# A hybrid decoder layer on one Trainium2 core: key preparation in two halves, gram masks with priority, side steps begun later, and one more dense unit in four chunk steps

## The chip, the cores and the metric

The program runs on one core of one Trainium2 chip. The core has five engines that work side by side, each through its own list of instructions in order: PE (TensorE: matrix products, with its weight loads PEld beside them), DVE (VectorE), ACT (ScalarE), POOL (GpSimd) and SP (SyncE, which here only issues transfers). They wait for one another by semaphores. Matrix products write to eight PSUM banks of 128 partitions by 512 fp32, everything else lies in SBUF. The metric is the time of one execution on the device in microseconds (us); lower is better.

## The reference, cut to what matters

One decoder layer, 512 tokens by 1024 channels in fp32, with a conditioning vector c that sets shifts, scales and gates:

```python
def rwkv7_time_mix(feat, ...):                    # group B, 8 heads of 64
    ...
    kk = kk / max(norm(kk), 1e-12)
    k = k * (1.0 + (a - 1.0) * k_a)
    def step(state, inp):
        r_t, w_t, k_t, v_t, kk_t, a_t = inp
        removed = einsum('bhvk,bhk->bhv', state, kk_t)
        state = state * w_t - removed * (kk_t * a_t) + v_t * k_t
        return state, einsum('bhvk,bhk->bhv', state, r_t)
    ...
# x1 = x + gate * (concat[fox_attention (A, 4 heads), rwkv7_time_mix (B), moba_attention (C, 4 heads)] @ w_out)
# all three from one projection of the normed and modulated x; then a gated MLP (width 2816) with a causal
# convolution of width 3, a gated residual add, and a last RMSNorm
```

## The kernel before

**Dense products.** Each fp32 matrix is split in a high and a low part, and a product is three matmuls of 128 x 512 (high by high, low by high, high by low; lines 459 to 461 for the input projection, 957 to 959 for the output projection). Three such matmuls are called a *dense unit* here. The class `Feed` holds the units of the input projection, and later of the output projection, as a queue. `feed.run(n)` puts the next n units at this place of the program, `feed.until(name)` as many as are needed for a named result. So units that depend on little stand between the steps of the recurrence, which depend on each other. Each unit also takes one *side step* from the list `feed.side` (line 115): 32 products of modulation weights on DVE (`mod2_steps`, line 434, each with a load of its own on SP's queue), then 16 more for the gates (`gate_steps`, lines 412 and 414) with their ends (`gate_parts`, lines 420 and 421; `gate_end`, lines 425 and 427).

**Order.** PE's instructions run in the order in which the code is written. On DVE, ACT and POOL a scheduler sets the order beforehand, by its own estimate of when an operand is ready and by priorities; `tc.high_priority(offset=n)` raises the operations inside it. On the chip each engine then keeps that order.

**Group B, gram stage (89.3 to 126.3 us).** The recurrence is worked in 8 chunks of 64 tokens, with the heads in four pairs j. For each pair `norm_cols(j)` spreads norms to a PSUM bank of the kind "at" (PE, line 529), `k_prep(j)` makes the key tiles from them on DVE (kk line 632, a 636, KR 637, BK 639, sq 641, BK 642, KR 643), `r_prep` (PE, line 665) and `k_cols` (POOL 653, ACT 655, PE transposes 658) use these, and `grams(j, par)` forms two products (PE, line 672), one in a bank "at" and one in a bank "ch". DVE multiplies each by a causal mask into AG (line 674, called the masks here), which frees the bank. There are 2 banks "at" and 3 "ch". Between the two grams of a pair stand F1 = 1 unit, behind them F2 = 2, 2, 2, 0 units. `norm_cols(j+2)` and `k_prep(j+2)` are written after the first gram of pair j.

**Chunk stage (185.5 to 269 us).** The loop over `cc` in `rwkv` carries the state `vs` through eight chunk steps. In each: px and py (PE, lines 1092 and 1098, which need the state), a softmax step of the attention and a unit ("a1"), pu (1108), copied back to `vs` by ACT (1109) and DVE (1110), again "a1", pn (1118), from which DVE makes the state of the next chunk in two additions with mp (line 1121; mp is POOL's, line 1102), the products of line 1124, and one unit. The attention steps put scores (1001, or 1003 and 1004, with 1005) in a bank "at", take their maximum on DVE (1008), exp on ACT (1010), 1011 and 1012 on DVE, then PE transposes (1019, in a bank "mm", like the units' sums) and ACT or DVE copies (1021). Operands of MoBA's scores are made in `split_head` (mqb line 732, mk line 735, on DVE). `scores` asks by `feed.until` for the units that it depends on.

**After that** the group norm (`gn_apply`), the rest of the attention, `put_y` (high part ACT line 936, low part POOL line 937), the output projection and, from 345 us on, the MLP, in which PE is never long without work.

Of the kernel before, what the change touches and what calls it, by code (L numbers as in the profile page):

```python
# [14 lines left out]
OP = mybir.AluOpType  # L15
# [3 lines left out]
P = 128  # L19
# [35 lines left out]
PAT = ['a1', 'a1', '1', '']  # L55
# [12 lines left out]
KO = 1  # L68
MP = ['', '2', '2']
PT = 3  # L70
GE = 3

SEVEN = (7, 9, 11, 13, 15)
NA = 16
# [66 lines left out]
def hybrid_trunk(ctx, tc, x, vecs, convs, mod_cols, mod_gates, in_first, in_cols, in_fox, in_moba, fox_f_bias, lora,  # L141
# [3 lines left out]
    V, S, G = nc.vector, nc.scalar, nc.gpsimd  # L145
# [4 lines left out]
    def c3(ap):  # L150
        return ap.rearrange("p (c t) -> p c t", t=C)
# [340 lines left out]
    with mix:  # L492
# [38 lines left out]
        with tc.tile_pool(name="prep", bufs=1) as pp:  # L531
# [98 lines left out]
            def k_prep(j):  # L630
                kk[j] = pp.tile([P, T], F32, name="kk", bufs=1)
                V.scalar_tensor_tensor(kk[j], kt[j], col("k_k", j), pnr[j], op0=OP.mult, op1=OP.mult)
                t1 = pp.tile([P, T], F32, name="t1", tag="sq", bufs=SQ)
                S.activation(t1, av[j], AF.Identity, scale=col("k_a", j), bias=omka[:, j:j + 1])
                G.tensor_tensor(kt[j], kt[j], t1, op=OP.mult)
                V.tensor_tensor(av[j], av[j], kk[j], op=OP.mult)
                V.tensor_tensor(KR[:, j, :, 0, :], c3(kk[j]), Pv[j][:, :, 0:64], op=OP.mult)
                BK[j] = pp.tile([P, 8, 3, 64], F32, name=f"BK{j}")
                V.tensor_tensor(BK[j][:, :, 0, :], c3(av[j]), c3(sv[j]), op=OP.mult)
                rk[j] = pp.tile([P, T], F32, name="sq", bufs=SQ)  # L640
                V.scalar_tensor_tensor(c3(rk[j]), KR[:, j, :, 1, :], col("r_k", j), c3(kt[j]), op0=OP.mult, op1=OP.mult)
                V.tensor_tensor(BK[j][:, :, 1, :], c3(kt[j]), c3(sv[j]), op=OP.mult)
                V.tensor_tensor(KR[:, j, :, 1, :], KR[:, j, :, 1, :], Pv[j][:, :, 1:65], op=OP.mult)
                S.copy(BK[j][H[1], :, 2, :], BK[j][H[1], :, 0, :])
# [22 lines left out]
            def grams(j, par):  # L667
                r = slice(64 * par, 64 * par + 64)
                for q in range(2):
                    pg = bank("ch" if q else "at", [P, 4, 2, 64])  # L670
                    for z in range(4):
                        mm(pg[:, z, :, :], BK[j][r, 4 * q + z, par:par + 2, :], KR[r, j, 4 * q + z, :, :],
                           start=True, stop=True)
                    V.tensor_tensor(AG[:, par, j, 4 * q:4 * q + 4, :].rearrange("p c (a t) -> p c a t", a=2), pg,
                                    mask[:, None, :, :].to_broadcast([P, 4, 2, 64]), op=OP.mult)

                for blk in range(2):
                    b = block(par, blk)
                    S.copy(AA[b, j], AG[b, par, j, :, 32 * blk:32 * blk + 32])


            norm_cols(0)
            k_prep(0)
            feed.until("r3")
            feed.run(LEAD[0])
            norm_cols(1)
# [3 lines left out]
            for j in range(4):  # L690
# [3 lines left out]
                k_cols(j, 0)  # L694
                for n, step in enumerate((lambda: grams(j, 0), lambda: feed.run(F1), lambda: k_cols(j, 1),
                                          lambda: grams(j, 1), lambda: feed.run(F2[j]), lambda: None)):
                    if n == KO and j < 2:
                        norm_cols(j + 2)
                        k_prep(j + 2)
                    step()  # L700
# [376 lines left out]


        v_tiles(0)
        feed.side += mod2_steps(w_m) + [mod2_end]  # L1080
        for half in range(2):
            feed.side += gate_steps(0, half, macc2, w_m) + [lambda half=half: gate_parts(0, half, m_part)]
            feed.side += [lambda: None] * GE + [lambda half=half: gate_end(0, half, bank("at"), g1b)]
# [1 line left out]
        for cc in range(NC_):  # L1085
# [42 lines left out]
            if cc > 5:  # L1128
                bonus(2 * cc - 12)
                bonus(2 * cc - 11)  # L1130
            fill(PAT[3])
        turn_bank[0] = "ch"
        gn_var(0)
        feed.run(G1)
# [443 lines left out]
```

## Time and profile before

| | |
|---|---|
| time, median of 3 runs | 745.96 us (744.57 to 748.39) |
| time of the profiled execution | 745.82 us |
| its span in the trace | 744.0 us, so 1.8 us lie around it |
| mean granted TensorE clock | 0.978 of full |
| PE, DVE, ACT, POOL busy in the span | 716.1, 484.3, 365.0, 311.6 us |

Busy time of PE holds waits that matmuls have inside them and stretches of slow clock, so that 96% isn't 96% of its peak. Idle time of another engine costs only what PE waits for it. The granted clock of a stretch stands in the column PEclk: 1.00 is 2.4 GHz, 0.50 is 1.2 GHz. In the rows by stretch that follow below, behind the stretch and its length stand PE, PEld, DVE, ACT and POOL, each as busy us and (x instructions), then PEclk, the share of the transfer engines and GB/s.

### The profile page before, as it was taken

To read this page: it belongs to the slowest core of one execution; us is meant where nothing else is said; L and a number is where in the kernel's file an instruction comes from. 1 tells how busy PE (TensorE), PEld (TensorE's weight loads), DVE (VectorE), ACT (ScalarE), POOL (GpSimd) and SP (SyncE) were. 2 spreads that over 40 slices of the span, in tenths; PEclk is the share of its full clock that TensorE was granted. 3 is DMA by queue.
4 is the path that set the end of the run, shared out by engine and by line. 5 is a ranking of instruction groups with operands and counts; after the bars stand their busy time and mean duration, and the time that the engine had idled before them with its cause. 6 is when DMAs were issued, how large, how long until landed. Compare 5 with 4: busy or idle time off the path is not lost.

```text
span 744.0 us, 11850 instructions
## 1 busy us (share of the span) xinstructions
PE 716.1 (96%) x4404; PEld 570.2 (77%) x4404; DVE 484.3 (65%) x833; ACT 365.0 (49%) x714; POOL 311.6 (42%) x264
## 2 busy tenths in 40 slices
PE   7999999999997999999999999999999999999996
PEld 5874767897665766677788888888888888888884
DVE  7957996876987567742639796788757683114104
ACT  8748655454432553645566545565563353223204
POOL 0023854664442312636576745454475432225210
PEclk9999989999977999999999999999999999999998
DMA  8941201237754141115234314323156633322203
GB/s 329 399 156 42 69 19 30 86 100 231 239 170 143 35 152 44 57 52 172 74 102 126 114 28 111 104 93 92 43 141 199 215 100 109 99 87 97 102 1 113
DMA packets 43021, 86.93 MB, mean 117 GB/s; under 512 B 5002, under 2 KB 5204, under 8 KB 42964
## 3 DMA queue, kind: packets, MB, share of 16 engines
q1 hardware_dynamic: 42963, 86.18, 36.0%
q8 instruction: 34, 0.56, 0.3%
q14 instruction: 24, 0.19, 0.1%
HBM read 84.05 MB, written 2.10 MB: 116 GB/s over the span
## 4 chain that ended last, share of the span: by engine, by line
PE 69%; DVE 15%; ACT 6%; issue 4%; POOL 3%; DMA 2%; SPq 0%; ACTq 0%; POOLq 0%; DVEq 0%
PE mm L459 3%; PE mm L460 3%; PE mm L461 2%; PE ch L378 2%; POOL w_lo L231 2%; PE ch L1188 2%; PE ch L1189 2%; PE ch L1187 2%; PE at L1315 2%; PE ch L1315 2%; PE at L1318 2%; PE at L1316 2%; DMA w_st<-in_w_up_dram 2%; PE ch L1318 2%; PE ch L1316 2%
## 5 line engine op out<-in xcount | busy, mean ns | idle before, releaser
L231 POOL TENSOR_TENSOR w_lo<-w_st,w_hi 128x512 fp32r<-128x512 f32 (+1 forms) x162 | 225.4, 1400 | 322.7 <-ACT w_hi L229 299.6
L229 ACT CAST w_hi<-w_st 128x512 fp32r<-128x512 f32 (+1 forms) x199 | 121.6, 618 | 157.1 <-PE at L1189 46.1
L231 DVE TENSOR_TENSOR w_lo<-w_st,w_hi 128x512 fp32r<-128x512 f32 x39 | 32.4, 832 | 72.8 <-ACT w_hi L229 72.7
L459 PE MATMUL mm<-h_hi,w_hi 128*128 128x512 f32 x104 | 49.4, 475 | 1.4 <-ACT ptr L1021 1.4
L460 PE MATMUL mm<-h_lo,w_hi 128*128 128x512 f32 x104 | 42.6, 410 | 0.0
L461 PE MATMUL mm<-h_hi,w_lo 128*128 128x512 f32 x104 | 42.6, 410 | 0.0
L1315 PE MATMUL ch<-h_hi,w_hi 128*128 128x512 f32 (+1 forms) x100 | 35.4, 363 | 0.7 <-ACT tm L1378 0.7
L1316 PE MATMUL ch<-h_hi,w_lo 128*128 128x512 f32 (+1 forms) x100 | 35.2, 361 | 0.0
L434 DVE SCALAR_TENSOR_TENSOR w_m<-w_m,cB 128x512 f32<-128x512 f32 x32 | 27.6, 886 | 9.3 <-DMA w_m<-in_mod_cols_dram 9.2
L1315 PE MATMUL at<-h_hi,w_hi 128*128 128x512 f32 (+1 forms) x88 | 32.4, 375 | 0.2 <-ACT tm L1378 0.2
L1316 PE MATMUL at<-h_hi,w_lo 128*128 128x512 f32 (+1 forms) x88 | 32.2, 372 | 0.0
L1008 DVE TENSOR_REDUCE mx<-at 128x1 f32<-128x128 f32 (+3 forms) x32 | 15.6, 488 | 18.9 <-PE at L1005 18.7
L1010 ACT ACTIVATE pr<-at,mx 128x128 f32<-128x128 f32 (+3 forms) x32 | 16.9, 527 | 21.8 <-DVE mx L1008 21.3
L459 PEld LDWEIGHTS mm<-h_hi,w_hi 128*128 128x128 f32 x104 | 20.6, 198 | 8.9 <-issue 3.1
L1444 ACT ACTIVATE tm<-tm 128x512 f32<-128x512 f32 x22 | 13.9, 632 | 27.5 <-DVE tm L1439 27.5
L1315 PE MATMUL mm<-h_hi,w_hi 128*128 128x512 f32 (+1 forms) x72 | 27.2, 382 | 0.0
L1316 PE MATMUL mm<-h_hi,w_lo 128*128 128x512 f32 (+1 forms) x72 | 27.1, 380 | 0.0
L461 PEld LDWEIGHTS mm<-h_hi,w_lo 128*128 128x128 f32 x104 | 20.6, 198 | 5.0
L1318 PE MATMUL ch<-h_lo,w_hi 128*128 128x512 f32 (+1 forms) x100 | 24.1, 363 | 0.0
L460 PEld LDWEIGHTS mm<-h_lo,w_hi 128*128 128x128 f32 x104 | 20.8, 200 | 2.4
L1445 DVE TENSOR_TENSOR tm<-tm 128x512 f32<-128x512 f32 x22 | 21.9, 993 | 1.0 <-ACT tm L1444 0.4
L1318 PE MATMUL at<-h_lo,w_hi 128*128 128x512 f32 (+1 forms) x88 | 22.2, 374 | 0.0
(667 smaller groups left out, 2049.3 us busy)
## 6 DMA issues: line engine op xcount, KB each, us to landing
w_st<-in_w_up_dram SPq DMA_DIRECT2D x88, 256.0 KB, 2.6
w_st<-in_w_down_dram SPq DMA_DIRECT2D x44, 256.0 KB, 2.6
wm<-in_mod_cols_dram SPq DMA_DIRECT2D x16, 512.0 KB, 10.3
w_m<-in_mod_cols_dram SPq DMA_DIRECT2D x32, 256.0 KB, 3.8
w_st<-in_in_cols_dram SPq DMA_DIRECT2D x30, 256.0 KB, 2.7
w_m<-in_mod_gates_dram SPq DMA_DIRECT2D x16, 256.0 KB, 2.9
w_st<-in_w_out_dram SPq DMA_DIRECT2D x16, 256.0 KB, 2.7
tm<-in_mod_gates_dram SPq DMA_DIRECT2D x16, 256.0 KB, 4.6
```

The costliest lines, as they stand in the source:

```text
L229: (V.tensor_copy if hv[0] else S.copy)(hi[:, :n], st[:, :n])
L231: e.tensor_tensor(lo[:, :n], st[:, :n], f32(hi[:, :n]), op=OP.subtract)
L434: V.scalar_tensor_tensor(wm, wm, 1.0, cB[:, cols], op0=OP.mult, op1=OP.mult, accum_out=acc2[:, z, k, half:half + 1])
L459: mm(out[0], hi[:, z, :], hT_hi[:, k, :], start=k == 0, stop=False)
L460: mm(out[0], hi[:, z, :], hT_lo[:, k, :], start=False, stop=False)
L461: mm(out[0], lo[:, z, :], hT_hi[:, k, :], start=False, stop=k == NK - 1)
L1008: V.reduce_max(mx[:, 0:1], s_ps[:, :n], axis=AX.X, negate=True)
L1010: S.activation(pr[:, :n], s_ps[:, :n], AF.Exp, bias=mx[:, 0:1], accum_out=mx[:, 1:2])
L1315: mm(o, hi[:, k, :], x[0][k], start=start and k == 0, stop=False, skip_group_check=not start)
L1316: mm(o, lo[:, k, :], x[0][k], start=False, stop=False, skip_group_check=not start)
L1318: mm(o, hi[:, k, :], x[1][k], start=False, stop=k == 3, skip_group_check=not start)
L1445: V.tensor_tensor(uv, ug, uv, op=OP.mult)
```

## The change

It does four things, and adds or removes no instruction:

1. `k_prep` is cut in two. kk, a and the first KR stay in it; BK, sq, the second BK, the second KR and the ACT copy become `k_prep2`. In the loop over the pairs `k_prep2(j+1)` is written after the first gram of pair j, and `norm_cols(j+2)` with the first half of pair j+2 ahead of the last units (n == 4), after the second gram.
2. The masks of line 674 get a priority offset of 60.
3. `feed.side` begins with 12 empty steps, so the 32 + 16 products are tied to units 12 places later.
4. Chunk steps 0 to 3 end with one more unit of the queue.

```diff
+AGP = 60
+SD = 12
...
                 V.tensor_tensor(KR[:, j, :, 0, :], c3(kk[j]), Pv[j][:, :, 0:64], op=OP.mult)
+
+            def k_prep2(j):
                 BK[j] = pp.tile([P, 8, 3, 64], F32, name=f"BK{j}")
...
-                    V.tensor_tensor(AG[:, par, j, 4 * q:4 * q + 4, :].rearrange("p c (a t) -> p c a t", a=2), pg,
-                                    mask[:, None, :, :].to_broadcast([P, 4, 2, 64]), op=OP.mult)
+                    with tc.high_priority(offset=AGP):
+                        V.tensor_tensor(AG[:, par, j, 4 * q:4 * q + 4, :].rearrange("p c (a t) -> p c a t", a=2), pg,
+                                        mask[:, None, :, :].to_broadcast([P, 4, 2, 64]), op=OP.mult)
...
             norm_cols(0)
             k_prep(0)
+            k_prep2(0)
...
-                    if n == KO and j < 2:
+
+                    if n == KO and j < 3:
+                        k_prep2(j + 1)
+                    if n == 4 and j < 2:
                         norm_cols(j + 2)
                         k_prep(j + 2)
...
-        feed.side += mod2_steps(w_m) + [mod2_end]
+        feed.side += [lambda: None] * SD + mod2_steps(w_m) + [mod2_end]
...
-            fill(PAT[3])
+
+            fill("1" if cc < 4 else PAT[3])
```

In the changed kernel the lines stand 2 to 10 lower (mask 674 is 679, pn's addition 1121 is 1130, the units 459 to 461 are 461 to 463).

DVE in the gram stage, from the first masks on. Before, two masks (AG) are followed by the seven products of pair 2's keys (kk to KR) and a product for kv, and only then by the masks of the second gram of pair 0:

```order
L674 TENSOR_TENSOR AG<-at,mask 128x512
L674 TENSOR_TENSOR AG<-ch,mask 128x512
L632 SCALAR_TENSOR_TENSOR kk<-kv,vec_107,at 128x512
L636 TENSOR_TENSOR a_731<-a_731,kk 128x512
L637 TENSOR_TENSOR KR<-kk,P_772 128x8x64
L639 TENSOR_TENSOR BK_945<-a_731,s_730 128x8x64
L641 SCALAR_TENSOR_TENSOR sq<-KR,vec_107,kv 128x512
L642 TENSOR_TENSOR BK_945<-kv,s_730 128x8x64
L643 TENSOR_TENSOR KR<-KR,P_772 128x8x64
L511 SCALAR_TENSOR_TENSOR kv<-mm,vec_107,kv 128x511
L674 TENSOR_TENSOR AG<-at,mask 128x512
L674 TENSOR_TENSOR AG<-ch,mask 128x512
```

In the changed kernel, the same place:

```order
L679 TENSOR_TENSOR AG<-at,mask 128x512
L679 TENSOR_TENSOR AG<-ch,mask 128x512
L679 TENSOR_TENSOR AG<-at,mask 128x512
L513 SCALAR_TENSOR_TENSOR kv<-mm,vec_107,kv 128x511
L679 TENSOR_TENSOR AG<-ch,mask 128x512
L634 SCALAR_TENSOR_TENSOR kk<-kv,vec_107,at 128x512
L638 TENSOR_TENSOR a_731<-a_731,kk 128x512
L639 TENSOR_TENSOR KR<-kk,P_772 128x8x64
L679 TENSOR_TENSOR AG<-at,mask 128x512
L643 TENSOR_TENSOR BK_1013<-a_731,s_730 128x8x64
L679 TENSOR_TENSOR AG<-ch,mask 128x512
L645 SCALAR_TENSOR_TENSOR sq<-KR,vec_107,kv 128x512
```

The masks of the second gram moved ahead of pair 2's products, and those of pair 1 stand between them. What lies ahead of these rows is as before: pair 1's seven products still precede the first mask. On PE the norms' matmul (line 529) of pairs 2 and 3 moved from the first unit between the two grams of a pair to behind the second gram.

PE from the end of chunk step 3 to the first score of step 4. Before, step 3 ends with one unit, and step 4 runs two units that `scores` asks for (mk_2432 comes out of the projection):

```order
L459 MATMUL mm<-h_hi,w_hi 128x512
L460 MATMUL mm<-h_lo,w_hi 128x512
L461 MATMUL mm<-h_hi,w_lo 128x512
L1092 MATMUL ch<-vs,AG 64x64 x8
L1098 MATMUL ch<-KR,vs 64x64 x8
L459 MATMUL mm<-h_hi,w_hi 128x512
L460 MATMUL mm<-h_lo,w_hi 128x512
L461 MATMUL mm<-h_hi,w_lo 128x512
L459 MATMUL mm<-h_hi,w_hi 128x512
L460 MATMUL mm<-h_lo,w_hi 128x512
L461 MATMUL mm<-h_hi,w_lo 128x512
L1003 MATMUL at<-mk_2432,mq_2152 128x128
```

In the changed kernel (mk_2352 is the same tile under another number):

```order
L461 MATMUL mm<-h_hi,w_hi 128x512
L462 MATMUL mm<-h_lo,w_hi 128x512
L463 MATMUL mm<-h_hi,w_lo 128x512
L461 MATMUL mm<-h_hi,w_hi 128x512
L462 MATMUL mm<-h_lo,w_hi 128x512
L463 MATMUL mm<-h_hi,w_lo 128x512
L1101 MATMUL ch<-vs,AG 64x64 x8
L1107 MATMUL ch<-KR,vs 64x64 x8
L1012 MATMUL at<-mk_2352,mq_2118 128x128
```

Step 3 now ends with two units and step 4 runs none ahead of its score. Steps 0, 1 and 2 also end with two where they had one, so the input projection is two units ahead from step 4 on. Behind the stage the output projection begins one attention step earlier, and two units fewer stand between the last attention products (1033) and the last units of the output projection.

DVE around the two additions that end chunk step 3. Before (macc are the gates' side steps, pr and mx the softmax):

```order
L1011 RECIPROCAL mx<-mx 128x1
L1121 TENSOR_TENSOR vs<-ch,mp 64x256
L1012 TENSOR_SCALAR pr<-pr,mx 128x512
L1121 TENSOR_TENSOR vs<-ch,mp 64x256
L414 SCALAR_TENSOR_TENSOR macc<-w_m,cact,macc 128x512 x3
L420 CAST m_part<-macc 128x512
L421 TENSOR_TENSOR m_part<-macc,m_part 128x512
L735 TENSOR_TENSOR mk_2432<-mm,mk_2432 64x512
```

In the changed kernel:

```order
L1020 RECIPROCAL mx<-mx 128x1
L1130 TENSOR_TENSOR vs<-ch,mp 64x256
L1021 TENSOR_SCALAR pr<-pr,mx 128x512
L744 TENSOR_TENSOR mk_2352<-mm,mk_2352 64x512
L1130 TENSOR_TENSOR vs<-ch,mp 64x256
L416 SCALAR_TENSOR_TENSOR macc<-w_m,cact,macc 128x512
L744 TENSOR_TENSOR mk_2355<-mm,mk_2355 64x512
```

The first mk product moved ahead of the second addition. In steps 0 to 3 the side steps moved little: 14 of the 32 products of line 434 stand ahead of the first maximum (1008) in both kernels, and at the copy of line 1110 in step 1 two more stand ahead of it than before.

## Rows read from the trace of the kernel before

**Rows 1.** The page: busy us by engine, share of the span, instructions.

```profile
PE 716.1 (96%) x4404; PEld 570.2 (77%) x4404; DVE 484.3 (65%) x833; ACT 365.0 (49%) x714; POOL 311.6 (42%) x264
```

**Rows 2.** Busy time by stretch: gram stage, then chunk steps 2, 3 and 4.

```profile
89.30:126.30 37.00, 34.18 (x230) 24.75 (x229) 31.72 (x39) 18.91 (x39) 19.31 (x15) 0.91 0.12 32
...
201.30:214.30 13.00, 12.20 (x101) 8.04 (x101) 10.28 (x25) 3.43 (x9) 5.84 (x6) 0.61 0.47 155
214.30:226.50 12.20, 10.21 (x122) 7.06 (x121) 11.99 (x26) 5.01 (x13) 6.79 (x9) 1.00 0.57 176
226.50:243.30 16.80, 14.40 (x121) 10.55 (x121) 12.64 (x24) 4.30 (x11) 3.76 (x4) 0.70 0.40 125
```

**Rows 3.** Busy time by stretch, the four that ran at the lower clock.

```profile
97.50:104.20 6.70, 6.70 (x19) 3.91 (x17) 6.60 (x8) 4.00 (x8) 2.73 (x2) 0.50 0.16 40
203.30:213.40 10.10, 9.34 (x68) 6.05 (x66) 7.46 (x19) 2.67 (x7) 3.69 (x4) 0.50 0.53 176
227.20:230.50 3.30, 3.30 (x22) 2.60 (x22) 3.11 (x5) 0.38 (x1) 1.44 (x2) 0.50 0.60 174
234.00:240.70 6.70, 6.27 (x39) 4.76 (x40) 4.16 (x10) 1.66 (x6) 0.00 (x0) 0.50 0.48 156
```

**Rows 4.** Timeline of PE, gram stage: start, duration, in brackets the wait before.

```profile
93.27 0.39 PE L460 MATMUL mm<-h_lo,w_hi 128*128 128x512 f32 x1
93.50 0.39 PE L461 MATMUL mm<-h_hi,w_lo 128*128 128x512 f32 x1
94.28 0.89 PE L658 MATMUL ch<-ident,BKs 64*128 64x64 f32 x8 [0.39 <-POOL BKs L653]
96.64 1.36 PE L672 MATMUL at<-KR,BK 64*128 64x128 f32 x8 [1.46 <-DVE AG L674]
...
100.23 0.63 PE L460 MATMUL mm<-h_lo,w_hi 128*128 128x512 f32 x1
...
115.17 1.16 PE L672 MATMUL ch<-KR,BK 64*128 64x128 f32 x8 [0.97 <-DVE AG L674]
```

**Rows 5.** Timeline of DVE, gram stage: a mask, and the next one.

```profile
96.50 0.68 DVE L674 TENSOR_TENSOR AG<-ch,mask 128x512 f32<-128x512 f32 x1
...
104.24 0.68 DVE L674 TENSOR_TENSOR AG<-at,mask 128x512 f32<-128x512 f32 x1
```

**Rows 6.** Waits of PE from 185 to 253 us: total, times, longest.

```profile
PE ch L1092 <- DVE vs L1121: 3.1, 4, 1.3
PE at L1003 <- DVE mk L735: 1.7, 1, 1.7
PE mm L459 <- ACT ptr L1021: 1.4, 2, 0.8
```

**Rows 7.** Timeline of PE, chunk stage: the state and a transpose in step 2, then waits behind step 3.

```profile
201.34 0.68 PE L1092 MATMUL ch<-vs,AG 128*64 128x64 f32 x14 [0.74 <-DVE vs L1121]
...
203.43 0.63 PE L1019 MATMUL mm<-ident,pr 128*128 128x128 f32 x2
...
225.53 0.30 PE L1092 MATMUL ch<-vs,AG 128*64 128x64 f32 x2 [1.34 <-DVE vs L1121]
226.48 0.68 PE L1092 MATMUL ch<-vs,AG 128*64 128x64 f32 x14 [0.65 <-DVE vs L1121]
```

**Rows 8.** Timeline of DVE and POOL, chunk stage.

```profile
194.19 1.10 DVE L434 SCALAR_TENSOR_TENSOR w_m<-w_m,cB 128x512 f32<-128x512 f32 x1
...
196.28 0.69 DVE L434 SCALAR_TENSOR_TENSOR w_m<-w_m,cB 128x512 f32<-128x512 f32 x1
...
192.64 2.10 POOL L1102 TENSOR_TENSOR mp<-vs,PC 64x256 f32<-64x256 f32 x2
```

**Rows 9.** Timeline of PE and POOL, a score and the first unit of the output projection.

```profile
299.06 0.91 PE L1001 MATMUL at<-fk,fq 66*128 66x384 f32 x2
...
300.92 0.50 PE L959 MATMUL mm<-w_hi,h_lo 128*128 128x512 f32 x1 [0.20 <-POOL h_lo L937]
...
300.14 6.09 POOL L937 TENSOR_TENSOR h_lo<-KR,h_hi 128x256 fp32r<-128x256 f32 x8
```

## The prediction

> **What bounds the kernel now.** I read the busy times first [rows 1]: PE works in 716.1 of 744.0 us, no other engine in more than 484.3. So a change that adds no instruction can only win what PE waits or loses to the lower clock, and both lie in few places. The busy time by stretch, with its clock column, then shows where: of the stretches that the change touches, the gram stage ran at a mean clock of 0.91, chunk step 2 at 0.61, step 4 at 0.70, and step 3 at 1.00 [rows 2]. Within these I looked for the stretches at exactly 0.50; there are four [rows 3]. What the lower clock does is seen in the same matmul of a unit: 0.39 us at 93.27, 0.63 at 100.23 [rows 4]. These times overlap with the next one: at full clock the next starts 0.23 us later (93.50), so a unit of three is worth about 0.7 us. Since half the clock takes twice the time for the same columns, I take half of the PE time in a stretch at 0.50 as lost.
>
> The list of waits then says what PE stood for. In the gram stage these are 0.39, 1.46 and 0.97 us [rows 4], 2.8 together. In the chunk stage they are 3.1 for the state of the next chunk (line 1121), 1.7 for mk and 1.4 for a softmax copy of ACT [rows 6], 6.2 together. The low stretches begin right behind such waits: the first after 0.39 and 1.46 in quick succession, the third after 1.34 and 0.65 [rows 3, 4, 7]; the wait of 0.97 at 115.17 was followed by no fall. So a wait costs itself, and sometimes several microseconds of half speed behind it. The clock cost 6.70 / 2 = 3.35 in the gram stage and (9.34 + 3.30 + 6.27) / 2 = 9.5 in the chunk stage [rows 3]. All that the change could win in these two stages is therefore 2.8 + 3.35 + 6.2 + 9.5 = 21.9 us.
>
> The Trainium skill, page TensorE: Matmul & The Clock Gate, Part 1, says that for modelling the ramp penalty is under 1% of a typical kernel span. By it the clock would be worth at most 7.4 us here; the four stretches show 12.8, and the sum goes by the stretches.
>
> **Gram stage: masks first.** At 96.64 PE waits to write a gram into a bank "at" that the first mask must empty. The norms' matmul of line 529 held the other bank "at" in between; it now comes after the second gram. So the "at" half of that gram starts when its transposes are through, about 95.2 (94.28 + 0.89). Its "ch" half needs a bank which the mask at 96.50 frees at about 97.2 [rows 4, 5]; the first half runs to about 96.2, so some 1.0 us of wait stands where 1.46 was. The seven products of pair 1 still precede the first mask, so this wait doesn't go. Then the change does help: before, the masks of the second gram waited behind pair 2's products from 97.2 to 104.24 [rows 5], and PE filled the time with units at half speed. Now they go at once, and the later ones stand between the products. The wait at 115.17 is of this kind too; I take its 0.97 as gone.
>
> The sum has 0.97 + 0.46 = 1.4 for the waits, and for the clock between 0 and 3.35: 0.39 and 1.0 stand behind each other, which lies between the 0.97 that passed and the 0.39 with 1.46 that did not. I take 0.6 of it, 2.0, and so a gain of **3.4 us** (1.2 to 4.8). More can't be had: DVE has 31.72 us of work in these 37.0 [rows 2], and a stage of 32.2 would leave it no room. What is late next is pair 2's own key products, which the masks now push back; POOL, with 19.31 us busy, covers that.
>
> The forward substitution that follows on DVE starts from the last masks and so moves with the stage; PE has units all through it. So the gain is not given back there.
>
> **Chunk stage: one more unit in steps 0 to 3.** A unit costs nothing as such, since it is taken from a later place. It is worth what it covers at the step's end, 0.7 us at full clock. Step by step:
> - Step 0: no wait there before; no gain.
> - Step 1: the two additions let PE wait 3.1 - 1.99 = 1.1 in all [rows 6, 7]; the unit covers 0.7, and as the rest was two short waits I count 0. But two more products of 0.69 [rows 8] stand ahead of the copy of line 1110, about 0.5 of a new wait before pn.
> - Step 2: the transposes of the softmax (1019) now want the bank that the second mqb product must empty. PE got to them 2.1 us after the second addition gave it the state (201.34 to 203.43) [rows 7]. Behind that addition DVE now has 1012, two mqb products and between them two of line 434; these take about 3.5 us, four at 0.69 (for mqb I take the duration of a product of line 434, which has as many columns) [rows 8] and 0.7 for 1012 and what POOL slows. So PE waits 1.4. Of the waits for copies (1.4 in two) I leave 0.4 here.
> - Step 3: DVE is the bound, 11.99 of 12.20 us busy [rows 2]. PE waited 1.99 [rows 7]. It gets there earlier if step 2 runs faster, and the mk product, taken at 0.69 like mqb, now stands between the two additions. The unit's 0.7 and this 0.69 cancel; for the earlier arrival I add 0.8, 2.8 in all. So the wait that the unit should hide grows where no DVE work goes away.
> - Step 4: the 1.7 for mk is gone, since that product comes early; PE's second copy wait stays at about 0.4.
>
> The waits after are 0.5 + 1.4 + 0.4 + 2.8 + 0.4 = 5.5, against 6.2. The clock decides: before it fell three times. In step 2 it fell behind waits which the unit largely covers, in step 4 a second time behind 1.7, which goes. A fall after step 3's 2.8 remains likely. I take about 8 us of PE time at 0.50, or 4.0 lost against 9.5. The gain is 0.7 + 5.5 = **6.2 us**; from 0.7, if all three falls stay, to 10.5, if none does and waits shrink no further.
>
> The rows bear on DVE's speed too. Beside POOL's products of line 1102 (2.10 for two) a product of line 434 takes 1.10 instead of 0.69 [rows 8], so about 0.4 each is lost when side steps lie there; the change leaves nearly as many there, so I count nothing. The Trainium skill, page SBUF — State Buffer, on the shared port pair, says that the loser fully blocks for the whole instruction. By it VectorE would stand still for the 2.10 and each such step would come 0.9 us later; the rows show both going on, slowed.
>
> **Side steps 12 places later.** The order of DVE shows almost the same products at the same places, because DVE and the loads set them, not the units. SP's loads of weights come a little earlier against these products' own loads. Cost and gain nothing; if the loads did come late, a product (0.69) would be late with them, which is inside the bounds of the chunk stage.
>
> **Tail.** Two units fewer stand at the output projection's start and end. Its first third matmul waited 0.20 for the low part from POOL [rows 9]. One attention step now stands behind that unit, of which the score alone takes 0.91, so PE gets there about 1 us earlier, while POOL's eight products there take 6.09 us from the same start [rows 9]. So the wait becomes 0.6 to 1.3, and with about 0.3 at the last unit I take a loss of **1.2 us** (0.3 to 2.5).
>
> **Sum.** Against the profiled execution: 745.82 - 3.4 - 6.2 + 1.2 = **737.4 us**. That execution lies 0.14 below the median of 745.96, so nothing is added for it.
>
> **Rivals.**
> - *No fall of the clock is left.* The chunk stage then gives 10.5, the gram stage 4.8, the tail costs 0.6: 731.1. For it: all falls stood behind waits over 1.1 us and most of these get shorter. Against: 2.8 in step 3.
> - *DVE bounds the chunk steps, so the units only move PE's waits.* DVE is busy 11.99 of 12.20 in step 3 and 12.64 of 16.80 in step 4 [rows 2]. PE then waits as long as before, the clock falls in steps 2 and 3, the stage gives about 1 and the gram stage 3.4 with a tail of 1.2: 742.6, at the edge of no change.
> - *Slower: the tail loses its cover.* The units moved forward are missing where the output projection waits for POOL. If that wait comes to more than about 1.5 us, as the waits that preceded a fall did, the clock falls there; a stretch such as those of 3.30 to 9.34 [rows 3] costs 1.7 to 4.7, with the wait 6. With the new bank wait in step 2 opening a second stretch (4.7) and only 1.4 won in the gram stage, and 1.7 for mk, the time is about 745.8 + 6 + 4.7 - 3.1 = 753. It decides from a tail wait of 1.5 on.
> - *The order doesn't do what it says.* The delay of the side steps is of that kind; if the masks too came no sooner, since the first one still waits behind seven products, only the chunk stage would pay: 745.82 - 6.2 + 1.2 = 740.8.
>
> **How the numbers follow.** A difference under 0.5%, 3.7 us, can hardly be told from none here; the borders are 742.2 and 749.7. Chances: my forecast (733 to 741) 0.47; no fall left 0.14; masks no help, at 740.8, 0.10; DVE as the bound 0.19, of which a good half lies beyond 742.2; slower or mishap in the tail 0.10, of which 0.07 beyond 749.7. So faster is 0.78, no change 0.15, slower 0.07. For 8 in 10 the range leaves out the fastest of the second case and the slow one: 730.5 to 744.
>
> **What would show it.** Right: in the gram stage masks between the key products, the wait at the second gram about 1.0 and for a "ch" bank, no 0.97 at pair 2, the stage near 33.5 us; in the chunk stage no wait for mk in step 4, full clock through step 2, and one fall behind step 3. Wrong: a stretch at 0.50 still from 97 on; waits at 1019 in step 2 over 2 us; a wait at line 1121's readers in step 3 well over 3 us; a low clock near 300 us; or DVE idle in steps 2 and 3, for then it is not the bound that I take it for.

## The result and the profile after

The changed kernel takes **737.69 us** (median of four, 735.14 to 739.35) against 745.27 for the kernel before in the same series; the ratio is 0.9889 (95% interval 0.9852 to 0.9926). A second series gave 738.86 and 0.9919 (0.9892 to 0.9946). So the gain is 0.8 to 1.1%, some 7 us, and the forecast of 737.4 was met. Its terms were not: that of the gram stage was 2.6 to 4 times too large, that of the chunk stage too small by 2.6 to 4.2 us.

The page of the changed kernel, engine times and the clock in 40 slices:

```profile
PE 709.4 (96%) x4404; PEld 565.1 (77%) x4404; DVE 479.2 (65%) x833; ACT 364.9 (50%) x714; POOL 310.5 (42%) x264
PEclk9999979999999999999999999999999999999999
```

All engines do the same work as in [rows 1]; PE is busy 6.7 us less for the same instructions. One dip of the clock is left, in the gram stage. The busy time by stretch (columns as in [rows 2]) shows the gram stage, then chunk steps 2, 3 and 4, then the only stretch at 0.50 between 60 and 360 us:

```profile
90.10:126.31 36.21, 35.35 (x230) 25.71 (x230) 30.77 (x39) 19.29 (x39) 19.32 (x15) 0.86 0.12 32
...
202.11:212.35 10.24, 9.15 (x107) 6.20 (x106) 9.99 (x25) 3.90 (x10) 5.95 (x6) 1.00 0.58 182
212.35:223.61 11.26, 10.82 (x120) 7.60 (x120) 10.99 (x26) 5.40 (x14) 5.14 (x8) 1.00 0.68 198
223.61:233.78 10.17, 8.73 (x116) 6.56 (x116) 9.85 (x20) 3.72 (x10) 4.75 (x6) 1.00 0.64 183
...
95.80:105.90 10.10, 10.04 (x37) 6.38 (x36) 7.28 (x10) 3.97 (x9) 4.54 (x3) 0.50 0.09 26
```

Against [rows 2, 3] the chunk steps run at 1.00, and steps 2 and 4 take 10.24 and 10.17 us instead of 13.00 and 16.80 (there the stretches were cut a little otherwise; from px to px, as cut here, they are 14.02 and 17.76). The gram stage is hardly shorter, and its stretch at 0.50 is longer than before: 10.10 us of which PE works 10.04.

The waits of PE from 185 to 253 us (total, times, longest), to be held against [rows 6]:

```profile
PE ch L1101 <- DVE vs L1130: 2.1, 4, 1.0
PE mm L1028 <- DVE mqb L741: 0.9, 1, 0.9
PE ch L1127 <- DVE vs L1119: 0.6, 1, 0.6
PE ch L1101 <- ACT vs L895: 0.5, 1, 0.5
PE ch L1107 <- DVE kv L923: 0.2, 1, 0.2
```

The waits for mk and for the softmax copies are gone, the two new ones (the bank behind mqb, the copy of line 1119 behind side steps) are there, and the state (line 1130, before 1121) costs 2.1 instead of 3.1.

To see where the time went I cut the span at five starts in the timeline of PE: first r_prep, first matmul after the grams, first px, last row of products (line 1124) of step 7, and the first matmul of the output projection's second half (line 966 before). For both kernels I have two profiles (the second ones are the control runs below):

| us | before | before, 2nd | after | after, 2nd |
|---|---|---|---|---|
| up to the gram stage | 89.31 | 89.80 | 90.10 | 89.50 |
| gram stage | 37.05 | 37.04 | 36.21 | 35.75 |
| up to the chunk stage | 59.16 | 59.16 | 59.16 | 59.16 |
| chunk stage | 81.94 | 79.05 | 72.97 | 71.64 |
| up to the output's second half | 74.67 | 74.64 | 74.29 | 75.29 |
| the rest | 401.87 | 401.81 | 403.77 | 402.06 |
| span | 744.0 | 741.5 | 736.5 | 733.4 |

The chunk stage gives 7 to 9 us although it now holds two units more (1.4 us), and the gram stage about 1. In the first profile the start and the rest, whose code the change leaves alone, take 2.7 of the gain back. The start varies by 0.8 us over all profiles, whatever the kernel. The rest isn't luck alone: in the four profiles of kernels without all four extra units (two of the kernel before, two of the experiments) it takes 401.7 to 402.1 us, in the ten with them 402.1 to 403.8. Each of these ten has a wait in the MLP that none of the four has, here that of the changed kernel:

```profile
PE mm L1236 <- DVE tm L1241: 0.3, 1, 0.3
```

So a small part of the gain is paid back there by the units; why the wait comes is open.

### The profile page after: what moved, and what is told of

The parts are those of the page before. It is cut to its first block, busy times and chain, and to the rows that moved or that the text cites. A ratio compares the mean times of both kernels' runs of the same rounds, so it can differ in the third digit from the quotient of the medians.

```text
span 736.5 us, 11843 instructions
## 1 busy us (share of the span) xinstructions
PE 709.4 (96%) x4404; PEld 565.1 (77%) x4404; DVE 479.2 (65%) x833; ACT 364.9 (50%) x714; POOL 310.5 (42%) x264
## 4 chain that ended last, share of the span: by engine, by line
PE 68%; DVE 13%; issue 5%; ACT 5%; DMA 4%; POOL 3%; SPq 0%; POOLq 0%; ACTq 0%; DVEq 0%
POOL w_lo L233 3%; PE mm L461 2%; PE ch L380 2%; PE ch L1198 2%; PE ch L1199 2%; PE ch L1197 2%; DMA w_m<-in_mod_cols_dram 2%; PE ch L1325 2%; DVE w_m L436 2%; PE mm L462 2%; PE at L1325 2%; PE ch L1328 2%; PE at L1328 2%; PE ch L1326 2%; PE at L1326 2%
## 5 line engine op out<-in xcount | busy, mean ns | idle before, releaser
L461 PE MATMUL mm<-h_hi,w_hi 128*128 128x512 f32 x104 | 47.5, 456 | 0.0
L436 DVE SCALAR_TENSOR_TENSOR w_m<-w_m,cB 128x512 f32<-128x512 f32 x32 | 27.1, 869 | 10.2 <-DMA w_m<-in_mod_cols_dram 10.0
L1325 PEld LDWEIGHTS ch<-h_hi,w_hi 128*128 128x128 f32 x100 | 18.8, 188 | 3.8 <-ACT tm L1388 0.6
```

Of the source, the lines that this page charges most:

```text
L436: V.scalar_tensor_tensor(wm, wm, 1.0, cB[:, cols], op0=OP.mult, op1=OP.mult, accum_out=acc2[:, z, k, half:half + 1])
L461: mm(out[0], hi[:, z, :], hT_hi[:, k, :], start=k == 0, stop=False)
L1325: mm(o, hi[:, k, :], x[0][k], start=start and k == 0, stop=False, skip_group_check=not start)
```

## The experiments

Each edit is to the changed kernel where nothing else is said. Times are medians, ratios are to the kernel before of the same series, whose medians were 744.87 to 746.17 us; a ratio need not be the quotient of the two medians.

**One part without the other: no extra unit.**

```diff
-            fill("1" if cc < 4 else PAT[3])
+            fill(PAT[3])
```

> The changed kernel with one unit at the end of chunk steps 0 to 3, as before; key halves, mask priority and delay stay. Theory (the extra unit made the chunk stage faster): only the gram stage's 0.8 us and the noise of the start are left, so 744 to 746; waits for the next state (line 1130) near 3 us in the chunk stage, and stretches at 0.50 in steps 2 to 4 again, 8 to 10 us lost. Rival (the gram stage's new order, or the delay, shifts the chunk steps out of the stalls): 737 to 739 with full clock in the chunk stage.

Measured: 740.69 us, ratio 0.9927 (0.9908 to 0.9946): neither 745 nor 738. In its profile step 4 (223 us on) is as bad as before, but step 2 ran at full clock without any unit:

```profile
200.03:210.29 10.26, 8.44 (x103) 5.68 (x103) 10.06 (x25) 4.09 (x11) 6.22 (x7) 1.00 0.58 194
222.20:240.29 18.09, 15.18 (x122) 10.87 (x122) 13.59 (x26) 4.21 (x11) 3.35 (x5) 0.62 0.42 128
...
PE ch L1101 <- DVE vs L1130: 3.3, 5, 1.3
PE mm L461 <- ACT ptr L1030: 1.8, 2, 1.1
PE at L1012 <- DVE mk L744: 1.6, 1, 1.6
```

So the waits of the stage came back as the theory of the unit has it. But more than half of the gain stayed (4.7 us against 745.34 in this series), which that theory hadn't.

**The extra unit alone**, put into the kernel before by the same line.

> The kernel before with the extra unit of chunk steps 0 to 3 alone. Theory of the unit: 736 to 739, chunk stage 73 us instead of 82 with no stretch at 0.50, gram stage 37 us as before with its waits of 1.46 and 0.97. Rival: 742 or more, falls of the clock in the chunk stage as before.

Measured: 740.93 us, ratio 0.9942 (0.9916 to 0.9968). Its chunk stage takes 75.6 us and its steps 2 and 4 look like those of the changed kernel:

```profile
207.62:217.57 9.95, 8.83 (x108) 6.01 (x107) 9.73 (x24) 3.91 (x10) 5.67 (x6) 1.00 0.56 184
228.81:238.99 10.18, 8.73 (x117) 6.56 (x116) 9.86 (x20) 3.72 (x10) 4.76 (x6) 1.00 0.59 185
```

In the chunk stage the unit does most of its work alone: 75.6 us against 81.9 and 79.1 before, and 73.0 and 71.6 in the changed kernel. PE still waits 2.0 us there for the copy of line 1110, where the changed kernel has 0.6 and 0.4. The product of the two ratios is 0.987, the ratio of the whole 0.989 to 0.992: the gain is the unit's and that of the other parts (called the gram part here), 4.4 and 4.7 us by the medians. Of the second, the profile without the unit shows some 1.7 us in the gram stage (35.39 against 37.05) and 1.1 between the chunk stage and the output's second half (73.54 against 74.67). There both profiles of the kernel before have two waits for the softmax that this one lacks:

```profile
PE ch L1019 <- DVE pr L1012: 0.6, 1, 0.6
PE ch L1019 <- DVE mx L1011: 0.5, 1, 0.5
```

The remaining 1.9 us aren't in a place that one profile shows.

**No delay of the side steps.**

```diff
-        feed.side += [lambda: None] * SD + mod2_steps(w_m) + [mod2_end]
+        feed.side += mod2_steps(w_m) + [mod2_end]
```

> The changed kernel without the 12 empty side steps. Theory (the delay moves next to nothing: on DVE only one addition of the gates changes its place, on PE two matmuls of the gates): 737.7 within 1.5, chunk stage 73 us at full clock. Rival (the delay takes side steps out of the crowded chunk steps): 740 or more with waits for the state over 3 us.

Measured: 736.52 us, ratio 0.9888 (0.9851 to 0.9926). The chunk stage takes 73.04 us with the same waits for the state (2.1). The 12 empty steps make no difference that is measured.

**No priority of the masks.**

```diff
-AGP = 60
+AGP = 0
```

> The changed kernel without the priority of the masks. By the order only two pairs of masks stand one product later and one mask changes place with a product of kv. Theory: no effect, 736.5 to 739, gram stage at equal clock as before within 0.3 us (32.2 us when 3.4 lost are taken off). Rival (the priority is what brings the masks forward): the wait of 0.97 at pair 2 returns, gram stage 1 us longer.

Measured: 736.84 us, ratio 0.9875 (0.9823 to 0.9927). The wait of 0.97 at pair 2 stays away; the gram stage keeps 0.8 and 0.9 of waits in pair 0. So it wasn't the priority that brought the masks forward; what is left is that pair 2's products are written after the second gram.

**Where the units stand, first: all four at the end of step 0.**

```diff
-            fill("1" if cc < 4 else PAT[3])
+            fill("4" if cc == 0 else PAT[3])
```

> The changed kernel with the four extra units all at the end of chunk step 0 and none at the ends of steps 1 to 3. Theory 1 (what counts is that the projection is two units ahead at step 4, so that mk is ready and no unit stands ahead of the scores): step 4 takes about 10 us as in the changed kernel (17.8 before), and the time is 737 to 739. Theory 2 (what counts is that a unit covers the wait for the state at the end of each step): waits for the state in steps 1 to 3 stay at 3 us, the clock falls in them, 740 to 742.

Measured: 745.50 us, ratio 0.9999 (0.9975 to 1.0023): the whole gain is gone, as much as the unit and the gram part bring together, though the gram stage takes 35.7 us in its profile. Neither theory had that. Its waits from 185 to 253 us, and steps 1, 3 and 4 by stretch:

```profile
PE mm L1028 <- DVE mqb L741: 3.9, 1, 3.9
PE mm L461 <- DVE mk L744: 2.8, 1, 2.8
PE ch L1101 <- DVE vs L1130: 0.8, 2, 0.4
...
193.84:207.10 13.26, 9.40 (x107) 7.02 (x106) 11.72 (x32) 4.95 (x15) 3.69 (x4) 0.87 0.73 234
216.20:231.24 15.04, 11.81 (x119) 8.15 (x118) 13.87 (x24) 6.09 (x15) 6.65 (x9) 0.89 0.50 142
231.24:239.96 8.72, 8.32 (x117) 6.30 (x116) 8.29 (x16) 3.14 (x9) 4.13 (x5) 1.00 0.33 93
```

Step 4 is faster still (8.72), as theory 1 says, but the projection's sums are finished before DVE can take them out of their banks "mm", and PE waits 3.9 and 2.8 for them in steps 1 and 3, whose mean clocks are 0.87 and 0.89. A unit that came before DVE could keep up was no filler here; it brought its tile's bank wait with it.

**Second: two units, at the ends of steps 2 and 3.**

```diff
-            fill("1" if cc < 4 else PAT[3])
+            fill("1" if cc in (2, 3) else PAT[3])
```

> The changed kernel with the extra unit at the ends of steps 2 and 3 alone, two instead of four; step 4 then needs none ahead of its scores. Theory 1 (two units ahead at step 4 is all): as the changed kernel within 1 us, step 4 about 10 us. Theory 2 (cover at each step's end): steps 1 and 2 wait about 1.1 and more again, the clock falls in step 2 in some executions, 739 to 741.

Measured: 738.40 us, ratio 0.9907 (0.9879 to 0.9936), between the two series of the changed kernel. Two units do what four do, within what is measured here. Step 4 took 14.53 us in its profile, with a wait of 1.8 for mk: not the 10 us of theory 1. By the profiles, chunk stage and the stretch up to the output's second half take 149.5 us together there, and 147.3 and 146.9 in the changed kernel, so the other two units may be worth 2 us there; the medians don't show it, and its rest (402.1 us) is among the short ones.

**The norms' matmul where it was**, with the key halves as changed.

```diff
+                    if n == KO and j < 2:
+                        norm_cols(j + 2)
                     if n == KO and j < 3:
                         k_prep2(j + 1)
                     if n == 4 and j < 2:
-                        norm_cols(j + 2)
                         k_prep(j + 2)
```

> The changed kernel with the norms' matmul (norm_cols of pairs 2 and 3) where it was, ahead of the unit between the grams; the key halves stay where the change put them. Theory (the matmul holds the bank at that the second gram wants): the wait for that bank returns, 1.2 to 1.5 us at the second gram of pair 0, and the wait for POOL falls from 0.8 to 0.4; the wait of 0.97 at pair 2 stays away. Gram stage 0.3 to 1 us longer at equal clock, 738 to 739. Rival (the order of masks and key products is all that counts): no wait over 1.1 there, same time as the changed kernel.

Measured: 737.85 us, ratio 0.9897 (0.9853 to 0.9941), as the changed kernel. The mechanism is as expected, seen in the waits of the gram stage:

```profile
PE at L676 <- DVE AG L679: 1.5, 1, 1.5
PE ch L662 <- POOL BKs L657: 0.4, 1, 0.4
```

The bank wait of 1.5 returns and the wait for POOL goes from 0.8 to 0.4, because this matmul (0.4 us) covered it. The sum is 1.9 either way, and the time is the same: its move bought nothing that is measured.

**Cover for POOL's wait: two units between the grams of pair 0.**

```diff
-                for n, step in enumerate((lambda: grams(j, 0), lambda: feed.run(F1), lambda: k_cols(j, 1),
-                                          lambda: grams(j, 1), lambda: feed.run(F2[j]), lambda: None)):
+                for n, step in enumerate((lambda: grams(j, 0), lambda: feed.run(F1 + (j == 0)), lambda: k_cols(j, 1),
+                                          lambda: grams(j, 1), lambda: feed.run(F2[j] - (j == 0)), lambda: None)):
```

> The changed kernel with two units between the grams of pair 0 and one behind, instead of one and two. Theory (the stretch at 0.50 from 95.5 to 106 follows the wait of 0.80 for POOL's BKs, and a unit of 0.7 covers it): wait under 0.2, no stretch at 0.50 in the gram stage, which takes about 31 us instead of 36.2; 732 to 733.5. Rival (the clock falls there for the small matmuls and the waits after them, whatever stands ahead): gram stage 35 to 37 us with a stretch at 0.50, 737 to 738.5.

Measured: 736.84 us, ratio 0.9890 (0.9864 to 0.9916), no gain over the changed kernel. The profile is of its longest execution (744.71 us, mean granted clock 0.982; the other nine had 0.986 to 0.995). In it the wait for POOL is gone, that of 1.1 for the first mask stays, and a stretch at 0.50 comes in which PE is busy throughout:

```profile
PE ch L676 <- DVE AG L679: 1.1, 1, 1.1
...
98.00:119.00 21.00, 21.00 (x83) 13.59 (x82) 12.20 (x17) 8.62 (x18) 5.05 (x6) 0.51 0.10 26
```

This profile doesn't tell what the other executions did. A mean clock of 0.986 over 739 us leaves at most 21 us at 0.50, and the last 2.4 to 4.9 us of every profile are of these, so none of the nine has room for a stretch that long; the three at 0.995 haven't even room for 6.8 us, the shortest seen in a gram stage. So in some executions the stretch was gone, and even these, at 733.67 to 735.66 us, didn't reach the 732 to 733.5 that the theory expected. But it was gone as well in one execution each of the run with the norms' matmul back (0.996) and of the unit alone (0.995), whose waits stand. So the cover isn't shown to be the reason.

**Both waits at once: a bank "mm" for the waiting half**, with the units as in the run above.

```diff
-                    pg = bank("ch" if q else "at", [P, 4, 2, 64])
+                    pg = bank(("mm" if j == 0 and par else "ch") if q else "at", [P, 4, 2, 64])
```

> The changed kernel with two units between the grams of pair 0 (one behind), and the second half of pair 0's second gram in a bank mm instead of ch, so that neither POOL's BKs nor the first masks let PE wait there. Theory (the stretch at 0.50 follows these two waits, 0.8 and 1.1): neither wait is left, no stretch at 0.50 in the gram stage, which takes 30 to 31 us; 733.5 to 735. Rival (the clock falls in the gram stage for the many small matmuls, or from wherever PE is held inside them): a stretch at 0.50 stays, the stage takes 33 us or more, the time stays within 1 of the changed kernel's 738.

Measured: 739.48 us, ratio 0.9940 (0.9905 to 0.9975). A miss: the extra unit finished a tile, and the bank "mm" was that tile's, whose product for kv waits on DVE. So it measured a longer wait in the same place, and a stretch at 0.50 of 23.5 us behind it (the profile is again of its longest execution, 747.41; the four at a mean clock of 0.979 to 0.981 took 745.0 to 747.4 us, the other eight, at 0.987 to 0.993, 736.8 to 740.1, with no room for such a stretch):

```profile
PE mm L676 <- DVE kv L513: 3.5, 1, 3.5
...
98.00:121.50 23.50, 21.82 (x82) 14.41 (x83) 12.37 (x17) 8.53 (x18) 4.88 (x5) 0.50 0.08 18
```

**Both waits at once, by units alone: one unit inside the second gram.**

```diff
                 for q in range(2):
+                    if q and par and j == 0:
+                        feed.run(1)
...
-                for n, step in enumerate((lambda: grams(j, 0), lambda: feed.run(F1), lambda: k_cols(j, 1),
-                                          lambda: grams(j, 1), lambda: feed.run(F2[j]), lambda: None)):
+                for n, step in enumerate((lambda: grams(j, 0), lambda: feed.run(F1 + (j == 0)), lambda: k_cols(j, 1),
+                                          lambda: grams(j, 1), lambda: feed.run(F2[j] - 2 * (j == 0)), lambda: None)):
```

> The changed kernel with the three units of pair 0 placed otherwise: two ahead of the second transposes (for POOL's BKs) and one between the two halves of the second gram (for the first masks), none behind. The banks stay as they are. Theory (the stretch at 0.50 follows the waits of 0.8 and 1.1): about 0.3 us of each wait is left, no stretch at 0.50 in the gram stage in the profile, stage 30.5 to 32 us, time 733.5 to 735.5. Rival (the fall comes from the stretch of small matmuls with holes inside them, or new waits at pair 1 whose BKs aren't ready open it): a stretch at 0.50 stays between 95 and 110, stage 34 us or more, 737 to 739.

Measured: 741.25 us, ratio 0.9943 (0.9922 to 0.9965), by the ratio behind the changed kernel's two series, though the intervals touch. On the waits it is yet the clearest answer. PE and POOL rows from its timelines, then two stretches:

```profile
97.44 1.16 PE L678 MATMUL ch<-KR,BK 64*128 64x128 f32 x8 [0.22 <-DVE AG L681]
...
101.41 1.05 PE L678 MATMUL ch<-KR,BK 64*128 64x128 f32 x8
...
110.72 0.76 PE L662 MATMUL ch<-ident,BKs 64*128 64x64 f32 x5 [2.14 <-POOL BKs L657]
...
107.80 1.41 POOL L233 TENSOR_TENSOR w_lo<-w_st,w_hi 128x520 fp32r<-128x520 f32 x1 [4.06 <-ACT w_hi L231]
109.17 1.49 POOL L657 TENSOR_TENSOR BKs<-BK,PC 128x512 f32<-128x512 f32 x1
...
94.50:110.70 16.20, 13.84 (x90) 9.47 (x90) 14.46 (x22) 9.72 (x21) 8.40 (x7) 1.00 0.09 20
111.20:124.80 13.60, 13.60 (x55) 10.27 (x55) 5.23 (x9) 5.36 (x11) 4.07 (x4) 0.50 0.01 4
```

With the two waits of pair 0 down to 0.22, the clock stays at 1.00 from 94.5 to 110.7, where it had fallen in every other profile. PE then reaches pair 2's transposes early and waits 2.14 for POOL, which has a weight's low part (w_lo) ahead of BKs in its order; for that part POOL had itself stood idle 4.06 us, until ACT had made the high part (w_hi). Behind this wait the clock falls to 0.50. So in this profile the small matmuls of pairs 0 and 1 ran at 1.00 without their waits, and the fall came behind a wait, as the theory said; but the wait only moved from pair 0 to pair 2. It is one profile.

**Controls: the changed kernel and the kernel before once more.**

> The changed kernel itself once more, for a second profile and more executions. If the stretch at 0.50 in the gram stage and its length (10.5 us) belong to the kernel, they return; if they vary from execution to execution, the gram stage takes another time (31 to 38 us) with other stretches, while its waits at full clock (0.8 for POOL and about 1.1 for the first mask) are the same. The chunk stage stays near 73 us at full clock either way.

> The kernel before once more, for a second profile. If the three stretches at 0.50 in its chunk stage belong to the kernel, they return and the stage takes 80 to 82 us. If that of step 2 varies (kernels without the extra unit there ran that step at full clock, 10.3 and 11.0 us), step 2 takes 10 to 11 us instead of 14.0, while step 4 stays at 17 to 18 us with its waits for mk. The gram stage has its waits of 1.46 and 0.97 in both cases.

The second profile of the changed kernel (spans in the table above) has the same two waits in full, since here the clock was still 1.00 when they came. The stretch at 0.50 came again behind them, but over 6.8 us:

```profile
94.48 0.89 PE L662 MATMUL ch<-ident,BKs 64*128 64x64 f32 x8 [0.81 <-POOL BKs L657]
95.21 1.11 PE L676 MATMUL at<-KR,BK 64*128 64x128 f32 x8
97.43 1.52 PE L676 MATMUL ch<-KR,BK 64*128 64x128 f32 x8 [1.11 <-DVE AG L679]
```

The second profile of the kernel before (743.51 us), by stretch: chunk steps 2 and 4.

```profile
200.93:211.17 10.24, 8.42 (x103) 5.70 (x104) 10.04 (x25) 3.89 (x11) 6.21 (x7) 1.00 0.56 185
223.10:240.87 17.77, 14.68 (x121) 10.72 (x122) 13.53 (x26) 4.31 (x11) 3.91 (x5) 0.71 0.43 129
```

Step 2 takes 10.24 us at full clock here, where the first profile had 14.02 with a stretch at 0.50; step 4 is slow in both. So the fall in step 2 comes in some executions, that in step 4 was there in all three profiles without the extra unit.

## Why the prediction came out right, by its steps

**Chunk stage: right in kind, too small.** Its gain was put at 6.2, with a fall left behind step 3. In the first two profiles the stage is 81.94 - 72.97 = 9.0 shorter with two units more in it, so the term is 9.0 + 1.4 = 10.4; by the second pair it is 7.4 + 1.4 = 8.8. The upper bound of 10.5 was added up wrong: 0.7 + 9.5 is 10.2. Two things were mis-sized. The wait behind step 3 was taken as 2.8, with a fall behind it; PE waited 0.41 there (and 1.03 behind step 4), and no fall came in the stage in either profile. The mk product does stand ahead of the second addition, and the two units cover it. But the 0.8 for an "earlier arrival" of PE was wrong, since DVE had less of its own ahead: before, its first addition began 2.15 us after pn ended, now 0.72. PE and DVE, before and after:

```profile
222.14 0.69 PE L1118 MATMUL ch<-vs,BKT 128*64 128x64 f32 x16
224.98 0.40 DVE L1121 TENSOR_TENSOR vs<-ch,mp 64x256 f32<-64x256 f32 x1
...
220.93 0.69 PE L1127 MATMUL ch<-vs,BKT 128*64 128x64 f32 x16
222.34 0.40 DVE L1130 TENSOR_TENSOR vs<-ch,mp 64x256 f32<-64x256 f32 x1
```

And the softmax copies, left at 0.4 each, cost nothing. The two new waits were found: 0.92 for the mqb bank (forecast 1.4) and 0.6 for the copy before pn (0.5). That DVE bounds step 3 was read rightly and led astray: DVE is busy 10.99 of 11.26 us there, but with the unit inside PE is busy 10.82 too, so the time was used.

That the units make step 4 short is shown: it takes 17.8 and 18.1 us in three profiles without them, 14.5 with two, 10.2 with one in each of four steps. It isn't the cover at the step's end that does it there: with all four at the end of step 0 it took 8.72. What counts for step 4 is that its two units and mk come earlier. For steps 1 and 2 no cause is shown: two units there make no difference that is measured.

**Gram stage: the step that failed.** Forecast 3.4, found 0.84 and 1.3. The masks did move, and the 0.97 at pair 2 is gone. But the 2.0 for the clock didn't come: a stretch at 0.50 is there in all seven profiles with this gram stage, as long as before (6.8 us) in five and 10.2 us in two, the first among them. What I hadn't priced is a wait: moving the norms' matmul away uncovers POOL's BKs, 0.39 becomes 0.80, and with 1.1 for the first mask, 1.9 us of wait stand in two pieces where 0.39 and 1.46 stood. In the first profile the fall comes right behind the 0.80, and at half speed PE then never meets the 1.1:

```profile
95.08 1.08 PE L662 MATMUL ch<-ident,BKs 64*128 64x64 f32 x8 [0.80 <-POOL BKs L657]
```

That "0.39 and 1.0" might pass without a fall was a guess between two rows; what stood there was more, and a fall followed in all seven. What I had said of POOL, that it covers pair 2's keys, was wrong as well: as soon as pair 0 doesn't wait, POOL's BKs are late.

**Delay: right as read from the order**, shown by the run without it. The priority had no term of its own in the sum; without it no difference is measured.

**Two readings of rows were wrong.** "All falls stood behind waits over 1.1 us" doesn't hold for step 2: there 0.35 and 0.74 stood ahead. And the rows of DVE beside POOL don't show "both going on, slowed". POOL's two products end at 192.64 + 2.10 = 194.74; a step of 0.69 that begins at 194.19 and stands still until then would end at 195.43, and it ended at 194.19 + 1.10 = 195.29 [rows 8]. So the rows can't tell turns from slowing, and the 0.9 us by which each step was to come later doesn't follow from them. Nothing in the sum rests on it.

**Tail: right in size, in part by luck.** Forecast 1.2 lost. From step 7 to the output's second half it takes 74.29 with two units fewer, 1.4, where it took 74.67, so 1.0 more; by the second pair it is 2.05. The 1.0 is the difference of two things, of which the prediction had one: without the unit the other parts shorten this stretch to 73.54, and from there the units cost 74.29 + 1.4 - 73.54 = 2.15 (0.8 from the kernel before to the unit alone). PE waits at the first units of the output projection, as [rows 9] suggested; waits of PE from 288 to 335 us:

```profile
PE mm L968 <- POOL h_lo L946: 0.5, 1, 0.5
PE mm L966 <- ACT h_hi L945: 0.4, 1, 0.4
PE ch L1028 <- DVE mx L1020: 0.4, 1, 0.4
```

In the second profile the clock falls right behind the first two (the tail is 1.0 longer there). So the rival that the tail loses its cover exists, at a fraction of its price, and its border of 1.5 us for a fall did not hold there.

**The sum** was right by luck: the errors of the gram stage (2.1 to 2.6 too much) and of the chunk stage (2.6 to 4.2 too little) nearly cancel, and the rest of the program, which had no term, took most of what was over in the first profile.

**Of the clock's share** the rule "half of the PE time at 0.50 is lost" was too simple. In step 2 of the kernel before, the fall costs 14.02 - 10.24 = 3.8 us by the two profiles, where the rule gives 9.34 / 2 = 4.7 [rows 3]. PE met a shorter wait at half speed, as the other engines went on meanwhile: 0.76 for a softmax copy at 0.50 and 1.08 at 1.00 (first and second profile):

```profile
204.83 0.80 PE L459 MATMUL mm<-h_hi,w_hi 128*128 128x512 f32 x1 [0.76 <-ACT ptr L1021]
...
205.46 0.49 PE L459 MATMUL mm<-h_hi,w_hi 128*128 128x512 f32 x1 [1.08 <-ACT ptr L1021]
```

Over 25 executions of the kernel before, the mean granted clock went from 0.977 to 0.991, and a straight line through them falls by 4.0 us for each 0.01, where 0.01 of 744 us is 7.4; over its other three series the line falls by 3.5, 4.8 and 5.6. On average the clock was 0.984 before and 0.991 in twelve executions of the changed kernel. By these lines that is 2.4 to 3.9 us of the gain, and the rest would be waits that are gone. This is an estimate: in the twelve the time hardly goes with the clock (738.7 and 739.0 us at 0.993, 735.3 and 736.8 at 0.990). By the same lines all that is missing to a clock of 1.00 in the kernel before would be worth 0.016 x 350 to 560 = 5.6 to 9.0 us, an estimate beyond the measured range (and 0.002 to 0.003 of the 0.016 lie at the very end of the program, where PE has nothing left to do); my first profile had shown 12.8. The Trainium skill, page TensorE: Matmul & The Clock Gate, Part 1, puts the ramp penalty below 1% of a typical kernel span, by estimate 7.4 us here. That is said of the low clock at a kernel's start, while the falls here come in its middle, so it doesn't price them; the average lies nearer to it than the profile that I preferred. Why a wait of about 1 us is followed by a fall in one execution and not in another stays open.

## What to carry to other kernels

Filler work helped here where it came early and spread one by one; the same four units in one place gave back everything, because their results wanted banks from the engine that was already full. Before moving an instruction away from a place, look at which wait it happens to cover: 0.4 us of matmul hid 0.4 us of POOL here. And take two or three profiles before a clock fall is priced: what shows in one may be there in every second execution.

## What the runs showed of the hardware that was not expected

The same program loses the clock in different places from one execution to the next. In step 2 of the kernel before it did so in one profile of two, behind waits of 0.35 and 0.74; in the other, waits of 0.46 and 0.74 passed. In the gram stage each of the four profiles of the two kernels has a stretch at 0.50, of 6.8 or 10.2 us; single executions of other runs, at a mean clock of 0.995 or 0.996, can't have had one of 6.8. Other runs have stretches of 21 us behind a wait of 1.1 and of 23.5 behind one of 3.5; in the first PE was busy all the time and the clock stayed at 0.50. The wait of 0.97 at pair 2 was followed by no fall in two profiles of the kernel before, and by one in the run with the unit alone (a second stretch at 0.50 there, and a gram stage of 40.17 us). The spread of the kernel's times (741.45 to 748.59 in 25 executions) goes with the mean granted clock.
